# Second products of logits and indexer scores over all 128 partitions

## The chip, the cores and the metric

The kernel runs on one core of a Trainium2 chip. The metric is the device time of one execution in microseconds (us); the time of the kernel before is the median of three runs. TensorE is called PE, VectorE DVE, ScalarE ACT, GpSimd POOL and SyncE SP; PEld is PE's loading of weights.

## The reference

One transformer block: a half feed-forward, a mix of two attentions with gates, another half feed-forward. 512 tokens, width 1024, 8 + 8 heads of 64, an indexer of 4 heads of 64. All is in float32. The part that the change touches is the dot products of queries and keys:

```python
dots = jnp.einsum('bqhd,bsd->bqhs', qib, k_idx_f) * (IDX_DIM ** -0.5)   # indexer, 4 heads
...
logits = jnp.einsum('bqhd,bqkhd->bqhk', qb, k_sel).astype(jnp.float32) * scale   # DSA, 8 heads
...
logits = jnp.einsum('bqhd,bqhjld->bqhjl', qc, k_g).astype(jnp.float32) * scale   # MoBA, 8 heads
```

q and k of both attentions are normalised per head (a root mean square over the 64 elements, times a gain). The indexer's scores select min(256, 512/4) = 128 keys for each query of the DSA attention.

## The kernel before, in words

Every float32 product is made of products of split numbers: a value is a high part (rounded to the short format that PE takes at full rate) and a low part (the rest). A 128-token tile of weights times activations thus takes three products, lines 118 to 120 in `mm3`.

The program goes through feed-forward 1, the mix, and feed-forward 2. PE's order is the order in which the code is written. DVE, ACT and POOL get their order from a scheduler, and then work through it strictly in turn. In the mix, `attention` is a generator that is woven with a *filler* (the projections of later pairs of heads, the gates): after each step of the attention the filler may put one to three `mm3` triples in between (`weave`). The MoBA attention (`br` = 1) runs first, with the indexer's scores (`score`) among its steps; then comes a phase with gates and branch products alone, during which DVE still selects the keys (`topk`); then the DSA attention (`br` = 0).

A step of an attention is a head and a tile of 128 queries (`qt` 0 to 3), 32 steps in each. `logits(i)` makes two products into one PSUM tile `s` (two buffers), line 577 and line 578. A head has 64 elements, so two heads share a tile of 128 partitions. In `q` each head has a slot of its own over all 128 partitions: the high part in the head's own half, the low part in the other half. `k` has the head's high part in both halves, so that line 577 sums q high times k high and q low times k high over 128 partitions. The keys' low parts `kl` lie with both heads in one tile, and line 578 takes one half of the partitions alone, of `q` and of `kl`. The columns are at least 256: 256 (qt 0 and 1), 384 or 512. Lines 503 and 504 do the same for the 12 scores, with `ki[0]` for line 577's `k` and `ki[1]`, which holds the low part in both halves, for `kl`.

What follows a logits tile is a chain over the engines: DVE adds the bias (L583), ACT takes the exponential (L75, through `table_op`), DVE takes the reciprocal and scales (L586, L587), PE transposes (L595, in `turn`, one step of `weave` later), ACT and DVE split the transposed tile (L603, L604), and PE multiplies with the values (L614, L615). DVE also makes the bias with the mask (L559), the selection (L523 to L527), the factors of the norms (L411 to L418, L438, L439) and the keys' low parts (L445). POOL splits the weights (L109).

Lines that the prediction names:

- L118, L119, L120: the three products of a weight tile, all over 128 partitions; L109: POOL's split of weights.
- L577, L578 (`logits`) and L503, L504 (`score`): the two products of each logits or score tile.
- L595: transposes of `turn`; L614, L615: products with the values.
- L445 (`k_post`): the keys' low parts; tag `kl`, two buffers, which gates 3 and 4 of the DSA mix take over later (L669 in `gate`).
- L534, L222: POOL's memsets at the start.

Of the kernel before, what the change touches and what calls it, by code (L numbers as in the profile page):

```python
# [16 lines left out]
P = 128  # L17
# [10 lines left out]
NF = F // P  # L28
# buffers; steps of the filler ahead of the attention (DSA, MoBA) and gates among the filler
TMPS, RAWS = 7, 3  # L30
AHEAD_A, AHEAD_B, GATES, GATES_B = 16, 12, 7, 3
# the step of the MoBA attention that the selection of each query tile follows; a score tile every so many steps
PIN, EVERY = (0, 20, 28, 31), 2
# steps from a product of k or q to the sums of its norm
LAG, LAG_Q = 11, 4
# products that keep the array busy at the start; how far the softmax goes before other work
SPIN, HURRY = 10, 200
# columns of w_in and its units of 128 of them, as kernel() lays them out
C_QA, C_KA, C_VA, C_QB, C_KB, C_VB, C_QI, C_KI, C_G = 0, 512, 1024, 1536, 2048, 2560, 3072, 3328, 3396
# [6 lines left out]
def f32(ap):  # L46
    return ap.bitcast(F32)
# [3 lines left out]
def block_kernel(ctx, tc, x, gains, wgu1, wd1, w_in, w_v, wb_a, wb_b, w_out, wgu2, wd2, rel_bias, onehot, out):  # L51
# [12 lines left out]
    def table_op(kind, *a, **k):  # L64
        """an activation whose table set is loaded once for all neighbours that it serves"""
        def after(prior, make):
            op = make()
            for x in prior:
                tc.add_manual_dep(op.ins, x.ins.name, NOSYNC, reason="table set")
            return op  # L70

        if group["kind"] != kind:
            prior, group["kind"], group["ops"], group["load"] = group["ops"][-16:], kind, [], None
            group["load"] = after(prior, lambda: nc.scalar.preload_act_table_set(kind))
        op = after([group["load"]], lambda: nc.scalar.activation(*a, **k))  # L75
        group["ops"].append(op)
        return op
# [24 lines left out]

# [1 line left out]
    def wtiles(n):  # L104
# [21 lines left out]
    def together(gens):  # L126
        """the products of several tiles, contraction tile by contraction tile"""
        for _ in zip(*gens):
            pass
        for g in gens:  # L130
            run(g)
# [18 lines left out]

# [1 line left out]
    ident = cp.tile([P, P], F32, name="ident")  # L152
# [5 lines left out]

    # keeps the array's clock up until the first data is there
    idle = tmp()[:, 0:P]  # L160
# [9 lines left out]
    nc.gpsimd.memset(epst, EPS)  # L170
    # columns QA, KA, QB, KB; q carries the scale 1/8 and a sign, k the -0.5 of its norm
    gqk = cp.tile([P, 4], F32, name="gqk")
# [6 lines left out]
    def rev(a):  # L179
        """the columns of a [128, 512] tile, back to front within each block of 128"""  # L180
        o = a[:, P - 1:P]
        return bass.AP(o.tensor, o.offset, [list(o.ap[0]), [P, NQ], [-1, P]])
# [5 lines left out]

# [1 line left out]
    def scaled(c, g0, src):  # L190
# [20 lines left out]
    def rsqrt_parts(v):  # L211
        """y near (v + eps)^-0.5 and b = (v + eps) y^2; the root is -0.5 (b - 3) y, one Newton step on."""
        y, b = tmp(), tmp()
        log_exp(y, v, AF.Ln, bias=epst)
        log_exp(y, y, AF.Exp, scale=-0.5)
        nc.scalar.activation(b, y, AF.Square)
        nc.vector.scalar_tensor_tensor(b, v, EPS, b, op0=ALU.add, op1=ALU.mult)
        return y, b
# [10 lines left out]

# [1 line left out]
    PARTS = ((0, 8), (8, 8), (16, 6))  # L231
# [3 lines left out]
    def ffn(xs, wgu, wd, after, lead, halves=whole):  # L235
        """lead() runs the products of the first tiles and returns the root of the norm"""
        tiles = []
# [36 lines left out]

# [1 line left out]
    xs1 = []  # L276
    ss1 = T("os", 1)

    def lead1(tiles, start, begun):
        """four tiles at once, as the parts of x and of the weights come in"""  # L280
        ws = []
# [23 lines left out]

# [1 line left out]
    tab = cp.tile([NB + 1, 16], F32, name="tab")  # L307
# [30 lines left out]

# [1 line left out]
    steps = [0]  # L340
# [52 lines left out]
    def q_post(p, gain, dst):  # L393
        """back to front by blocks and not normalised; a head's high part in its half of the partitions,
        its low part in the other; the norm's factors and their reciprocals, queries on partitions"""
        sq = tmp()
# [24 lines left out]
        later(LAG_Q, norm)  # L421

    def k_post(p, gain, dst):
        """a head's high part in both halves of the partitions, and the low parts of both heads in one more tile"""
        k1 = tmp()
        nc.vector.tensor_mul(k1, p, r2)
        sq = tmp()
        sh, sl = tmp(F32R), tmp(F32R)
        nc.scalar.activation(sh, k1, AF.Square)
        nc.gpsimd.tensor_mul(sq, k1, k1)  # L430
        nc.gpsimd.tensor_sub(sl, sq, f32(sh))

        def norm():
            p2 = mmps()
            nc.tensor.matmul(p2, bd, sh, start=True, stop=False)
            nc.tensor.matmul(p2, bd, sl, start=False, stop=True)
            y, b = rsqrt_parts(p2)
            nc.vector.scalar_tensor_tensor(b, b, -3.0, y, op0=ALU.add, op1=ALU.mult)  # L438
            nc.vector.tensor_mul(y, k1, b)  # L439
            k, low = T("k", 2, (P, 2, S), F32R), T("kl", 2, (P, S), F32R)  # L440
            for e, h1 in enumerate(HALF):
                g = gain[h1]
                for h2 in HALF[e], HALF[1 - e]:
                    nc.scalar.activation(k[h2, e, :], y[h1, :], AF.Copy, scale=g)
                nc.vector.scalar_tensor_tensor(low[h1, :], y[h1, :], g, f32(k)[h1, e, :],  # L445
                                               op0=ALU.mult, op1=ALU.subtract)
            dst.extend([k, low])

        later(LAG, norm)

    def v_units(br, j, dsts, bank=mmps):
        """v of two pairs of heads, tokens on partitions;
        [key tile][head of the pair] has 64 columns of high parts, then 64 of low ones"""
        vs = []
# [34 lines left out]

# [1 line left out]
    ki = [T("a", 16, (P, S), F32R) for _ in range(2)]  # L491
# [5 lines left out]
    def score(qt, hd):  # L497
        W = P * (qt + 1)
        acc = work[:, WOFF[qt]:WOFF[qt] + W]
        b = HALF[hd % 2]  # L500
        q = qi[hd][:, qt * P:(qt + 1) * P]
        p = sps()
        nc.tensor.matmul(p[:, 0:W], q, ki[0][:, 0:W], start=True, stop=False)  # L503
        nc.tensor.matmul(p[:, 0:W], q[b], ki[1][b, 0:W], start=False, stop=True)  # L504
        rl = tmp()
# [22 lines left out]

# [1 line left out]
    PTW = 1664  # L530
# [7 lines left out]
    def attention(br, pairs, outs, extra):  # L538
        """yields how many products of the filler may go in between"""
        sel = br == 0  # L540
# [9 lines left out]
        def addend(i):  # L550
            """bias and mask, over the factor that the sums of products still need"""
            if i < 32:
# [11 lines left out]
        def logits(i):  # L564
# [5 lines left out]
            e = hd % 2  # L570
            b = HALF[e]
            (q, f, _), (k, kl), _ = pairs[hd // 2]
# [4 lines left out]
            nc.tensor.matmul(p[:, 0:N], qb, k[:, e, 0:N], start=True, stop=False)  # L577
            nc.tensor.matmul(p[:, 0:N], qb[b], kl[b, 0:N], start=False, stop=True)  # L578
            addend(i + 1)
# [74 lines left out]

# [1 line left out]
    wide = []  # L656

    def gate(gi, keep):
        """kept until it is used, some of them where a pair of heads had its q or k"""
        def post(p):  # L660
            if gi in (3, 4):
                g1 = T("kl", 2)
            elif gi in (5, 6):
# [16 lines left out]

# [1 line left out]
    moba, dsa = ([([], [], []) for _ in range(4)] for _ in range(2))  # L682
# [21 lines left out]
    nc.vector.tensor_copy(r2T, p[:, 0:NQ])  # L704
    # of the queries, back to front, for both heads of a pair; and its square
    r2q = cp.tile([P, 2, 2 * NQ], F32, name="r2q")
# [56 lines left out]

# [1 line left out]
    def lead2(tiles, start, begun):  # L765
# [22 lines left out]
def _units(w, cols=None, n=P):  # L788
    """[rows, columns] as [unit of n columns, partition, rows of the unit by tiles of 128]"""
    cols = range(0, w.shape[1], n) if cols is None else cols  # L790
    return np.stack([w[:, c:c + n].reshape(-1, P, n).transpose(1, 0, 2).reshape(P, -1) for c in cols])
# [34 lines left out]
```

## Time and profile before

| | |
|---|---|
| median of 3 runs | 1178.36 us (1177.1 to 1178.37) |
| span of the profiled execution | 1176.5 us |
| PE busy | 1163.6 us (99%), 5356 products |
| DVE busy | 700.3 us (60%) |
| POOL busy | 532.4 us (45%) |
| ACT busy | 468.8 us (40%) |
| HBM | 92 GB/s over the span |

The page gives the span alone for the profiled execution, no time of its own; the runs lie 0.6 to 1.9 us above that span. A product's time in the trace runs from its start to a modelled end, and neighbours overlap; what a product costs PE is the distance from its start to the next one's start. "issue" after an idle time means that the engine waited for nothing that the profile shows. The attention stages lie between 420 and 541 us (MoBA) and between 613 and 730 us (DSA).

### The profile page before, as it was taken

What the parts mean: (1) busy time and instruction counts of PE and PEld (TensorE: products, weight loads), DVE (VectorE), ACT (ScalarE), POOL (GpSimd) and SP (SyncE); (2) the same over time, 40 slices, a digit from 0 to 9 for tenths busy, and PEclk for the clock granted to TensorE, in tenths of its full rate; (3) what the DMA queues carried; (4) which work ended last, traced back from release to release, by engine and by line L of the source; (5) the groups of instructions that cost most, each with busy time, mean ns of one, the idle gap of its engine ahead of it and who ended that gap; (6) DMA issues with size and microseconds to landing.
All of it is one profiled execution on the core that took longest, in us unless ns stands there. A gap on an engine that the chain in (4) does not pass through costs nothing.

```text
span 1176.5 us, 14070 instructions
## 1 busy us (share of the span) xinstructions
PE 1163.6 (99%) x5356; PEld 946.2 (80%) x5356; DVE 700.3 (60%) x1075; ACT 468.8 (40%) x757; POOL 532.4 (45%) x280
## 2 busy tenths in 40 slices
PE   9999999999999999999999999999999999999998
PEld 7778888888888878768877767778888888888887
DVE  5863165514655678799979896665665146622651
ACT  6422222312244667657337665433422223222221
POOL 2444454444544655654462422443554444544442
PEclk9999999999999999999999999989999999999999
DMA  7233323323233221221241221322323223232222
GB/s 233 93 109 91 107 90 100 97 92 106 81 83 105 99 82 46 88 63 55 89 135 63 75 69 36 101 96 90 108 90 99 98 90 108 90 104 93 92 88 90
DMA packets 38171, 109.59 MB, mean 93 GB/s; under 512 B 4214, under 2 KB 8664, under 8 KB 38104
## 3 DMA queue, kind: packets, MB, share of 16 engines
q1 hardware_dynamic: 37960, 108.67, 28.9%
q8 instruction: 42, 0.69, 0.2%
q14 instruction: 25, 0.20, 0.1%
q10 hardware_dynamic: 144, 0.02, 0.0%
HBM read 106.54 MB, written 2.14 MB: 92 GB/s over the span
## 4 chain that ended last, share of the span: by engine, by line
PE 93%; DVE 4%; issue 1%; POOL 1%; ACT 1%; DMA 0%; SPq 0%; POOLq 0%; ACTq 0%; DVEq 0%
PE mm L118 22%; PE mm L119 21%; PE mm L120 21%; PE s L118 7%; PE s L119 7%; PE s L120 7%; PE s L578 2%; PE pt L595 1%; PE o L614 1%; PE o L615 1%; PE s L577 1%; POOL wlo L109 1%; PE pt L408 0%; DVE fq L415 0%; DVE kl L445 0%
## 5 line engine op out<-in xcount | busy, mean ns | idle before, releaser
L109 POOL TENSOR_TENSOR wlo<-raw,whi 128x1024 fp32r<-128x1024 f32 (+2 forms) x199 | 467.1, 2349 | 532.1 <-ACT whi L108 529.8
L108 ACT ACTIVATE whi<-raw 128x1024 fp32r<-128x1024 f32 (+2 forms) x207 | 205.0, 993 | 529.3 <-PE mm L119 294.0
L118 PE MATMUL mm<-x,whi 128*128 128x512 f32 x632 | 258.8, 410 | 0.6 <-ACT whi L108 0.6
L120 PE MATMUL mm<-x,wlo 128*128 128x512 f32 x632 | 246.9, 391 | 0.0
L119 PE MATMUL mm<-x,whi 128*128 128x512 f32 x632 | 246.7, 390 | 0.0
L119 PE MATMUL mm<-a,whi 128*128 128x512 f32 (+1 forms) x462 | 178.7, 387 | 0.3
L118 PE MATMUL mm<-a,whi 128*128 128x512 f32 (+1 forms) x462 | 178.6, 386 | 0.0
L120 PE MATMUL mm<-a,wlo 128*128 128x512 f32 (+1 forms) x462 | 178.5, 386 | 0.0
L118 PEld LDWEIGHTS mm<-x,whi 128*128 128x128 f32 x632 | 118.8, 188 | 33.4 <-issue 7.5
L120 PEld LDWEIGHTS mm<-x,wlo 128*128 128x128 f32 x632 | 118.6, 188 | 26.1 <-DVE wlo L109 0.6
L118 PE MATMUL s<-x,whi 128*128 128x512 f32 x352 | 137.0, 389 | 0.6 <-ACT tmp L75 0.6
L119 PE MATMUL s<-x,whi 128*128 128x512 f32 x352 | 137.0, 389 | 0.0
L120 PE MATMUL s<-x,wlo 128*128 128x512 f32 x352 | 137.0, 389 | 0.0
L119 PEld LDWEIGHTS mm<-x,whi 128*128 128x128 f32 x632 | 118.9, 188 | 20.0 <-issue 0.5
L271 DVE SCALAR_TENSOR_TENSOR h<-mm,h 128x512 f32<-128x512 f32 (+1 forms) x49 | 33.3, 681 | 165.3 <-PE mm L120 165.3
L262 DVE TENSOR_TENSOR tmp<-tmp,tmp 128x512 f32<-128x512 f32 x44 | 99.0, 2250 | 29.6 <-ACT tmp L75 29.4
L146 DVE TENSOR_TENSOR a<-tmp,a 128x512 fp32r<-128x512 f32 x49 | 88.5, 1806 | 31.9 <-ACT a L145 31.8
L119 PEld LDWEIGHTS mm<-a,whi 128*128 128x128 f32 x462 | 86.8, 188 | 18.6 <-DVE a L146 1.1
L118 PEld LDWEIGHTS mm<-a,whi 128*128 128x128 f32 x462 | 86.9, 188 | 17.8
L120 PEld LDWEIGHTS mm<-a,wlo 128*128 128x128 f32 x462 | 86.8, 188 | 17.6
L562 POOL TENSOR_SCALAR l<-bias,fq 128x128 f32<-128x128 f32 (+3 forms) x40 | 42.8, 1073 | 78.8 <-PE pt L595 63.0
L118 PEld LDWEIGHTS s<-x,whi 128*128 128x128 f32 x352 | 66.0, 188 | 14.9 <-ACT tmp L75 1.0
(166 smaller groups left out, 1438.9 us busy)
## 6 DMA issues: line engine op xcount, KB each, us to landing
raw<-in_ffn_w_gu_dram SPq DMA_DIRECT2D x84, 512.0 KB, 3.4
raw<-in_w_in_dram SPq DMA_DIRECT2D x35, 512.0 KB, 3.4
raw<-in_ffn_w_down_dram SPq DMA_DIRECT2D x32, 512.0 KB, 3.6
raw<-in_ffn_w_down_dram SPq DMA_DIRECT2D x16, 384.0 KB, 3.1
bias<-fd SPq DMA_DIRECT2D x16, 256.0 KB, 3.4
raw<-in_w_v_dram SPq DMA_DIRECT2D x8, 512.0 KB, 3.4
raw<-in_w_out_dram SPq DMA_DIRECT2D x8, 512.0 KB, 3.4
h<-in_x_dram SPq DMA_DIRECT2D x8, 256.0 KB, 4.2
```

The source lines that it names most:

```text
L108: nc.scalar.activation(hi, raw, AF.Copy)
L109: eng.tensor_sub(lo, raw, f32(hi))
L118: nc.tensor.matmul(pt, wh, xh, start=start, stop=False)
L119: nc.tensor.matmul(pt, wh, xl, start=False, stop=False)
L120: nc.tensor.matmul(pt, wl, xh, start=False, stop=stop)
L146: nc.vector.tensor_sub(lo, src, f32(hi))
L262: nc.vector.tensor_mul(g1, g1, s)
L271: nc.vector.scalar_tensor_tensor(h[c][:, b], pd, 0.5, h[c][:, b], op0=ALU.mult, op1=ALU.add)
L562: nc.gpsimd.tensor_scalar(tms[i], b, inv, None, op0=ALU.mult)
L577: nc.tensor.matmul(p[:, 0:N], qb, k[:, e, 0:N], start=True, stop=False)
L578: nc.tensor.matmul(p[:, 0:N], qb[b], kl[b, 0:N], start=False, stop=True)
L595: nc.tensor.transpose(pp[:, kt * P:(kt + 1) * P], pe[:, kt * P:(kt + 1) * P], ident)
```

## The change

The keys' low parts get two tiles that stay for the whole program, `low0` and `low1`, with a slot of 512 columns for each head of a pair. POOL fills with zeros, once, the half of the partitions that is not the head's own. `k_post` takes the two tiles in turn and writes a head's low part into its half of its slot. The second product of `logits` then takes the head's whole slot of `q` and of `low`, and the second product of `score` takes the whole of `q` and of `ki[1]`, so that here q low times k low is added, which was not computed before. Gates 3 and 4 get a tag of their own, `g`, with two buffers. The memory set aside for the descriptors of dynamic DMAs is cut to 1024; what is left of the diff drops comments. Line numbers of the changed kernel are 6 or so higher than before.

```diff
@@
+    lows = [cp.tile([P, 2, S], F32R, name=f"low{i}") for i in range(2)]
+    for low in lows:
+        for e in range(2):
+            nc.gpsimd.memset(f32(low)[HALF[1 - e], e, :], 0.0)
+    turns = [0]
...
@@ k_post
-            k, low = T("k", 2, (P, 2, S), F32R), T("kl", 2, (P, S), F32R)
+            k, low = T("k", 2, (P, 2, S), F32R), lows[turns[0] % 2]
+            turns[0] += 1
...
-                nc.vector.scalar_tensor_tensor(low[h1, :], y[h1, :], g, f32(k)[h1, e, :],
+                nc.vector.scalar_tensor_tensor(low[h1, e, :], y[h1, :], g, f32(k)[h1, e, :],
@@ score
-        b = HALF[hd % 2]
...
-        nc.tensor.matmul(p[:, 0:W], q[b], ki[1][b, 0:W], start=False, stop=True)
+        nc.tensor.matmul(p[:, 0:W], q, ki[1][:, 0:W], start=False, stop=True)
@@ logits
-            b = HALF[e]
...
-            nc.tensor.matmul(p[:, 0:N], qb[b], kl[b, 0:N], start=False, stop=True)
+            nc.tensor.matmul(p[:, 0:N], qb, kl[:, e, 0:N], start=False, stop=True)
@@ gate
-                g1 = T("kl", 2)
+                g1 = T("g", 2)
@@ kernel
-    nc = bacc.Bacc("TRN2", target_bir_lowering=False, num_devices=1)
+    nc = bacc.Bacc("TRN2", target_bir_lowering=False, num_devices=1, dynamic_dma_scratch_size=1024)
```

PE, ACT and SP keep their order, instruction by instruction. Two places differ. On DVE, near the end of the DSA attention, the multiplication of gate 4 (`kl_6219`, then `g_6217`, out of the PSUM tile `mm`) stands among the softmax of the last two steps; `st` and `l` are the softmax's sums and rows. Before:

```order
L583 ISA l_6179,st_6207<-s_6202,l_6179,fq_5827 128x384
L583 ISA st_6207 128x1
L586 RECIPROCAL st_6207<-st_6207 128x1
L604 TENSOR_TENSOR pt_2634<-pt_6215,pt_2633 128x128
L587 TENSOR_SCALAR l_6179<-l_6179,st_6207 128x384
L583 ISA l_6205,st_6237<-s_6234,l_6205,fq_5827 128x512
L583 ISA st_6237 128x1
L669 TENSOR_TENSOR kl_6219<-mm_6141,R_2731 128x512
```

And in the changed kernel:

```order
L589 ISA l_6177,st_6205<-s_6200,l_6177,fq_5825 128x384
L589 ISA st_6205 128x1
L675 TENSOR_TENSOR g_6217<-mm_6139,R_2737 128x512
L592 RECIPROCAL st_6205<-st_6205 128x1
L610 TENSOR_TENSOR pt_2640<-pt_6213,pt_2639 128x128
L593 TENSOR_SCALAR l_6177<-l_6177,st_6205 128x384
L589 ISA l_6203,st_6235<-s_6232,l_6203,fq_5825 128x512
L589 ISA st_6235 128x1
```

The multiplication has moved five instructions ahead, from behind the bias of the last step to behind that of the step before it. On POOL, at the very start of the program, the zeros stand between the constants and the memsets of `pt`; this is the changed kernel:

```order
L170 MEMSET epst 128x1
L174 TENSOR_SCALAR gqk<-gT 128x1 x4
L308 MEMSET tab 33x16
L426 MEMSET low_2627 64x512 x2
L426 MEMSET low_2628 64x512 x2
L541 MEMSET pt_2637 128x128
L541 MEMSET pt_2638 128x128
L541 MEMSET pt_2639 128x128
L541 MEMSET pt_2640 128x128
L222 MEMSET tmp_307 128x128
L109 TENSOR_TENSOR wlo_336<-raw_334,whi_335 128x1024
```

Four memsets have come in, ahead of the memset of L222 and of the first split of weights; the rest of POOL's order is as it was.

## Rows read from the trace of the kernel before

**Rows 1.** Busy time by stretch of the attention: window, length, PE, PEld, DVE, ACT, POOL, clock
```profile
420.00:498.50 78.50, 78.40 (x399) 58.64 (x398) 61.62 (x157) 54.31 (x126) 47.18 (x34) 1.00 0.21 68
498.50:541.00 42.50, 41.97 (x198) 30.77 (x198) 40.74 (x120) 24.12 (x52) 25.17 (x18) 1.00 0.21 62
613.40:623.20 9.80, 9.80 (x45) 7.17 (x45) 8.11 (x21) 7.05 (x18) 3.00 (x2) 1.00 0.29 105
623.20:695.90 72.70, 69.20 (x367) 53.54 (x367) 67.37 (x161) 50.85 (x111) 28.51 (x17) 1.00 0.20 66
695.90:730.00 34.10, 34.10 (x162) 26.02 (x163) 25.67 (x65) 18.89 (x40) 7.79 (x4) 1.00 0.15 47
```
**Rows 2.** Chain of work that ended last, 672.8 to 696: start, us, what
```profile
673.32 2.15 DVE l L559
...
695.87 0.30 PE pt L595
```
**Rows 3.** Same stretches, instructions on the tile s alone: PE (x two per pair), PEld, DVE, ACT
```profile
420.00:498.50 78.50, 21.01 (x62) 11.50 (x62) 11.24 (x21) 4.18 (x10) 1.00 0.21 68
498.50:541.00 42.50, 9.13 (x26) 4.82 (x26) 6.18 (x11) 1.66 (x3) 1.00 0.21 62
613.40:623.20 9.80, 2.50 (x8) 1.29 (x7) 2.18 (x4) 0.00 (x0) 1.00 0.29 105
623.20:695.90 72.70, 13.53 (x40) 7.43 (x40) 10.12 (x19) 0.00 (x0) 1.00 0.20 66
695.90:730.00 34.10, 5.41 (x16) 2.96 (x16) 5.09 (x9) 0.00 (x0) 1.00 0.15 47
```
**Rows 4.** Line 578: its products in ns (min/median/max), PEld's idle time before its loads
```profile
L578 PE MATMUL s<-kl,q x64: 379/410/501, 420.7 to 721.8; 64*128 64x256 f32 x32, 64*128 64x384 f32 x16, 64*128 64x512 f32 x16
...
  issue: 16.5, 58
```
**Rows 5.** PE in order of time, a score tile and a logits tile: start, us, what
```profile
440.98 0.28 PE L503 MATMUL s<-a,a 128*128 128x256 f32 x1
...
441.83 0.39 PE L119 MATMUL mm<-x,whi 128*128 128x512 f32 x1
...
442.29 0.39 PE L577 MATMUL s<-k,q 128*128 128x512 f32 x1
442.62 0.49 PE L578 MATMUL s<-kl,q 64*128 64x512 f32 x1
443.04 0.50 PE L118 MATMUL mm<-x,whi 128*128 128x512 f32 x1
443.37 0.39 PE L119 MATMUL mm<-x,whi 128*128 128x512 f32 x1
```
**Rows 6.** PE in order of time, products with the values, two of each width
```profile
445.04 0.40 PE L614 MATMUL o<-pt,v 128*128 128x512 f32 x1
...
445.50 0.34 PE L614 MATMUL o<-pt,v 128*128 128x384 f32 x1
...
445.86 0.28 PE L614 MATMUL o<-pt,v 128*128 128x256 f32 x1
...
446.09 0.28 PE L614 MATMUL o<-pt,v 128*128 128x256 f32 x1
```
**Rows 7.** PEld in order of time, loads for the logits tile of rows 5
```profile
442.61 0.18 PEld L578 LDWEIGHTS s<-kl,q 64*128 64x128 f32 x1 [0.36 <-issue]
...
443.14 0.19 PEld L119 LDWEIGHTS mm<-x,whi 128*128 128x128 f32 x1
```
**Rows 8.** POOL in order of time, the start of the program
```profile
4.66 0.65 POOL L534 MEMSET pt<- 128x128 f32 x4
8.87 0.20 POOL L222 MEMSET tmp<- 128x128 f32 x1 [3.56 <-DVE os L204]
```
**Rows 9.** DVE in order of time, end of the DSA attention
```profile
717.36 0.75 DVE L559 SCALAR_TENSOR_TENSOR l<-bias,fq,work 128x512 f32<-128x512 f32 x1 [0.80 <-PE pt L595]
...
721.68 0.16 DVE L586 RECIPROCAL st<-st 128x1 f32<-128x1 f32 x1 [1.77 <-ACT l L75]
```

## The prediction

> **What bounds the kernel now.** I read first the busy time by stretch over the two attentions, since only there the edited products run. The reader is to see that PE is busy almost without a break: of the five stretches it idles 0.10, 0.53, 0, 3.50 and 0 us (length less busy time), at full clock [rows 1]. So a product that takes PE less time should bring the end forward by as much. But DVE is a close second. Its idle time in the same stretches is 16.9, 1.8, 1.7, 5.3 and 8.4 us [rows 1]. The chain of work shows what that means: from 673.32 to 695.87 us it starts on DVE and comes back to PE only at the end [rows 2], and almost all pieces between are DVE's. There PE was not the bound, it just had enough filler to look busy. I call the stretches A (420 to 498.5), B (498.5 to 541), C (613.4 to 623.2), D (623.2 to 695.9) and E (695.9 to 730). A and B are the MoBA attention, with B holding the selection on DVE; C to E are the DSA attention.
>
> **What the change takes off PE.** The tile s gets two products per logits or score tile, and PE has 62, 26, 8, 40 and 16 instructions on it in A to E [rows 3]: 31, 13, 4, 20 and 8 pairs, 76 in all, which are the 64 of L578 and the 12 of L504. What one pair costs is read from starts, not from durations: a 64-row product shows 379 to 501 ns, and PEld idles 16.5 us before 58 of its 64 loads, 0.28 us each [rows 4], but both overlap with neighbours. For a tile of 512 columns, from L577's start to the start of the product behind the next one it is 443.37 less 442.29, 1.08 us for three products (0.33, 0.42 and 0.33 us each) [rows 5]. Products over 128 rows with fresh weights each, two into one tile, step by (445.50 - 445.04) / 2 = 0.23 us at 512 columns, 0.18 at 384 and 0.115 at 256 [rows 6]. Three of 512 would take 0.69 us, so 0.39 us is lost: 0.10 on the way into the 64-row product, 0.19 at it, 0.10 behind the next. For a score tile of 256 columns it is 441.83 less 440.98 = 0.85 us [rows 5], against 2 x 0.115 + 0.23 = 0.46: again 0.39. Since the loss does not grow with the columns, I take it for 384 too. The second product over 128 rows has the form of L577 (type, weights, columns); zeros stream like other numbers. So PE is relieved of 76 x 0.39 = 29.6 us, in A to E 12.1, 5.1, 1.6, 7.8 and 3.1.
>
> The bound from below for this term is the load of weights. In rows 7 the load for L578 idles 0.36 us and starts at 442.61, beside its own product, while the load for L119 starts at 443.14, with L118's product of 443.04 [rows 5] still running over the same 128 rows. Loads ahead under full-height products are thus what this kernel does all the time, and I take the whole 0.39. The Trainium skill, page "TensorE: Matmul & The Clock Gate", section "Part 3: Packing small matmuls — row/col tiling", speaks against it: it says that a weight load overlaps products in flight only when its row group differs. The trace does not agree with that as it stands (rows 7). By that rule the second product's load would come into the open.
>
> **What it adds and moves.** Each of these I cost at nothing. The low parts are written by as many DVE instructions of the same shape, and the two tiles alternate as the two buffers of `kl` did, so L445 waits for the same logits as before; were it to wait longer, the softmax queued behind it on DVE would wait, and PE's transposes for that. The four memsets of 64x512: four of 128x128 take 0.65 us, 0.16 each, so one costs between that and four times as much for four times the columns, and all four 0.65 to 2.6 us; POOL then idles 3.56 us before L222, which waits for DVE [rows 8]. That idle time hides them; without it the start would slip by at most 2.6 us. Gate 4's multiplication moves ahead of a reciprocal (L586) that waited 1.77 us for ACT [rows 9]. It takes about the 0.75 us of a 128x512 DVE instruction [rows 9], and its own product ends three PE products (0.7 us) behind the logits of that step, so it fits into that wait. If not, it costs 0.75 us in the last steps' softmax, once. Gates 3 and 4 no longer wait for `kl`, which can only help; I give it nothing. The memory for dynamic DMAs concerns none, as the kernel issues its DMAs on SP and ACT.
>
> **What of 29.6 us reaches the end.** DVE's work stays the same, and the attention ties PE to it step by step, so a stretch cannot shrink by more than DVE's idle time and, since some of that is waiting for ACT inside the chain, not by all of it. D is my gauge: DVE idles 7% of it, and PE already idles 5%.
> - A: relief 12.1, DVE idle 16.9. Afterwards DVE would idle 4.8 of 66.4 us, 7% as in D, so PE would begin to wait; I take 10.5 (bounds 8 and 12.1).
> - B: relief 5.1, DVE idle 1.8, PE idle 0.5. DVE bounds it; I take 1.2 (0 and 5.1).
> - C: relief 1.6, DVE idle 1.7; I take 1.4 (1 and 1.6).
> - D: relief 7.8, DVE idle 5.3, and the chain on DVE for 22.5 us of it; I take 2.8 (0 and 7.8).
> - E: relief 3.1, DVE idle 8.4; I take it all (2 and 3.1).
>
> The sum is 10.5 + 1.2 + 1.4 + 2.8 + 3.1 = 19.0 us, with bounds of 11 and 29.7. Between the attentions and behind them PE finds what it found before, only earlier: DVE's selection comes earlier with the end of the MoBA attention. The sum is made against the span of 1176.5 us and gives 1157.5; the median of the runs lies 1.9 us above the span, so I predict 1178.4 - 19.0 = 1159.4 us.
>
> **Rivals.**
> - *DVE holds nothing back* (0.12): the softmax may lag behind by a step while PE goes on with filler, and DVE catches up after each attention. All 29.6 us arrive: 1148.8 us. For it: PE hardly idles in B although DVE is 96% busy. Against: the chain on DVE in D [rows 2].
> - *DVE holds more back* (0.13): the lower bounds, 11 us, give 1167.4 us, and it goes on to 1176 if A too is bound by DVE.
> - *The loads of weights come into the open* (0.04): the load takes 0.18 to 0.19 us [rows 7], so a pair wins 0.39 - 0.19 = 0.20 us, 15.2 us in all. DVE then takes less back; with the relief halved in A, C and E (6.2, 0.8, 1.6) and the same 1.2 and 2.8 in B and D it is 12.6 us: 1165.8 us. This is what the rule of that page of the Trainium skill would do here. Against it stand rows 7.
> - *The height is not the cause* (0.04): all slow products are at once 64 rows high and the second ones into s, and the pair could be slow for the other reason. Then nothing is won: 1178, or 1181 if the memsets show. Against it: L614 and L615 also go in pairs into one tile, without loss [rows 6].
> - *Slower, as DVE meets POOL more often* (0.05): L559 took 2.15 us in the chain of D [rows 2] and 0.75 in E, for the same shape [rows 9], 1.4 us more. The place is B and D, where POOL has 18 and 17 instructions [rows 1]. With DVE pressed closer, each of them might catch one more DVE instruction of the chain; it decides from 19.0 / 1.4 = 14 more such meetings on, and 20 more would give 1178.4 - 19.0 + 28 = 1187 us. Against it: DVE is already busy 93 to 96% there, and both engines have as many instructions as before. The Trainium skill, page "SBUF — State Buffer", section "Who interferes with whom", says that a DVE instruction with two SBUF inputs and a POOL instruction that reads SBUF block each other; L559 reads two SBUF tiles, and its row agrees with that.
>
> **How the numbers follow.** The forecast, DVE takes about a third back, 1153 to 1166 us, gets 0.62. The first rival's end is the lower end of the range, 1148.5; the upper end is 1168, just past the lower bounds of the sum, so that the part of "holds more back" above it (0.09), "not the cause" and "slower" are left out, 0.18. A measurement of this kernel can tell about 0.2% from no change, 2.4 us. Faster: 0.62 + 0.12 + 0.13 + 0.04 = 0.91; same 0.04; slower 0.05.
>
> **What would show it.** In the changed profile the second products show 128 rows and the duration of the first ones (0.39 us at 512 columns [rows 5]), the step of a 512 tile to the second product behind it falls from 1.08 to 0.69 us, and PEld's "issue" idle time before these loads is gone; if not, the height was not the cause. PE's idle time on DVE grows from 4 us by some 10, in A, B and D; if it stays, the first rival holds. Stretch E and the gates behind it should shift as a block. I am wrong if a product over 128 rows on the same tiles still steps like the 64-row one, or if DVE's own time in B and D changes by more than a few us.

## The result and the profile after

The changed kernel takes 1162.93 us (1162.74 to 1167.82, four runs) against 1178.36 us. The ratio is 0.9882, with a 95% interval of 0.9863 to 0.9901: 1.2% faster, 15.4 us. Forecast were 1159.4 us and a range of 1148.5 to 1168. The execution whose profile is shown here is the slowest of the four, 1167.82 us with a span of 1166.0 us, 5 us above the others: its mean granted clock was 0.992, theirs 0.998 to 0.999, and PE's clock fell in it at two places where it had not fallen in the profile of before (last section).

The products behave as forecast. PE in order of time, a score tile and a logits tile of the changed kernel, to be held against [rows 5]:

```profile
424.80 0.28 PE L510 MATMUL s<-a,a 128*128 128x256 f32 x1
...
425.27 0.39 PE L119 MATMUL mm<-x,whi 128*128 128x512 f32 x1
...
425.73 0.40 PE L583 MATMUL s<-k,q 128*128 128x512 f32 x1
425.96 0.39 PE L584 MATMUL s<-low,q 128*128 128x512 f32 x1
426.19 0.39 PE L118 MATMUL mm<-x,whi 128*128 128x512 f32 x1
426.42 0.39 PE L119 MATMUL mm<-x,whi 128*128 128x512 f32 x1
```

From the first product to the second one behind the tile it is 426.42 less 425.73 = 0.69 us (before 1.08), and 0.47 us for the score tile (before 0.85). PEld shows why nothing is left over:

```profile
425.50 0.19 PEld L583 LDWEIGHTS s<-k,q 128*128 128x128 f32 x1
425.73 0.19 PEld L584 LDWEIGHTS s<-low,q 128*128 128x128 f32 x1
```

The second product's weights are loaded from 425.73 on, while the first product, which starts at the same moment, runs over the same rows.

Then the busy time by stretch (columns as in [rows 1]), with the borders at the PE instructions at which A to E begin and end before:

```profile
420.00:489.30 69.30, 67.10 (x400) 58.22 (x399) 59.96 (x152) 52.34 (x122) 46.54 (x34) 1.00 0.23 77
489.30:529.50 40.20, 37.59 (x198) 30.88 (x197) 39.74 (x121) 24.43 (x54) 23.40 (x18) 1.00 0.21 66
604.40:612.70 8.30, 8.30 (x46) 7.05 (x46) 6.65 (x16) 6.67 (x17) 3.00 (x3) 1.00 0.34 122
612.70:688.50 75.80, 65.37 (x369) 55.33 (x367) 70.89 (x166) 50.64 (x112) 28.05 (x17) 0.95 0.20 63
688.50:719.50 31.00, 31.00 (x163) 26.05 (x162) 25.39 (x65) 18.39 (x40) 7.87 (x4) 1.00 0.17 52
```

A is 9.2 us shorter, B 2.3, C 1.5 and E 3.1, but D is 3.1 us longer, and the stretch between the attentions grew from 72.4 to 74.9 us: 10.5 in all, the difference of the two spans. The medians differ by 15.4; the clock that PE lost at those two places, some 5 us by the rows of the last section, makes up the rest (an estimate). PE, which idled 0.1, 0.5 and 3.5 us in A, B and D, now idles 2.2, 2.6 and 10.4. Who it waits for in the changed kernel (total in us, times, longest):

```profile
PE pt L601 <- DVE pt L610: 12.0, 10, 2.6
PE pt L601 <- DVE l L593: 1.8, 1, 1.8
...
PE pt L601 <- DVE st L592: 1.2, 1, 1.2
```

Nearly all of it is transposes of the softmax that wait for DVE, 15.0 us. In the kernel before it was 4.0 us:

```profile
PE pt L595 <- DVE pt L604: 2.6, 3, 1.9
PE pt L595 <- DVE l L587: 1.4, 1, 1.4
```

What DVE did then is seen where its rows stand beside POOL's. DVE in order of time in D of the changed kernel:

```profile
662.95 2.85 DVE L566 SCALAR_TENSOR_TENSOR l<-bias,fq,work 128x512 f32<-128x512 f32 x1
...
675.70 2.36 DVE L415 TENSOR_TENSOR fq<-fq 128x8 f32<-128x8 f32 x1
...
685.64 2.54 DVE L593 TENSOR_SCALAR l<-l,st 128x256 f32<-128x256 f32 x1
```

POOL in the same stretch:

```profile
662.88 2.38 POOL L109 TENSOR_TENSOR wlo<-raw,whi 128x1024 fp32r<-128x1024 f32 x1 [3.88 <-ACT whi L108]
...
675.63 2.40 POOL L109 TENSOR_TENSOR wlo<-raw,whi 128x1024 fp32r<-128x1024 f32 x1 [6.57 <-ACT whi L108]
...
685.66 2.36 POOL L109 TENSOR_TENSOR wlo<-raw,whi 128x1024 fp32r<-128x1024 f32 x1 [0.67 <-ACT whi L108]
```

Each DVE instruction begins within 0.1 us of a POOL split of weights and ends 0.03 to 0.54 us after it; that is what is called a meeting here. One of the three has only 8 columns; the form of the first, 512 columns, took 0.75 us elsewhere [rows 9]. Behind two of the three, PE then waits:

```profile
667.91 0.44 PE L601 MATMUL pt<-ident,l 128*128 128x128 f32 x1 [2.63 <-DVE pt L610]
...
688.32 0.41 PE L601 MATMUL pt<-ident,l 128*128 128x128 f32 x2 [1.79 <-DVE l L593]
```

DVE counts as busy while it is held, so its 93% of D (70.89 of 75.8 us) were not 93% of work. How much it is can be summed from the traces: over both attentions and what lies between them (420 us to the end of E), the DVE instructions that run beside a split and take over 0.2 us more than the shortest of their form lose 27.0 us (20 instructions) before and 30.6 us (21) in the changed kernel; in D alone 10.6 and 14.2 us, eight instructions each time. That is what the experiments go after.

### The profile page after: what moved, and what is told of

The parts are those of the page before. It is cut to its first block, busy times and chain, and to the rows that moved or that the text cites. A ratio compares the mean times of both kernels' runs of the same rounds, so it can differ in the third digit from the quotient of the medians.

```text
span 1166.0 us, 14074 instructions
## 1 busy us (share of the span) xinstructions
PE 1141.1 (98%) x5356; PEld 949.4 (81%) x5356; DVE 701.4 (60%) x1075; ACT 467.3 (40%) x757; POOL 532.8 (46%) x284
## 4 chain that ended last, share of the span: by engine, by line
PE 83%; DVE 9%; ACT 3%; issue 3%; POOL 1%; DMA 0%; SPq 0%; POOLq 0%; ACTq 0%; DVEq 0%
PE mm L120 20%; PE mm L118 20%; PE mm L119 20%; PE s L118 7%; PE s L119 7%; PE s L120 7%; DVE l L566 1%; DVE l L589 1%; POOL wlo L109 1%; DVE l L593 1%; DVE pt L610 1%; PE pt L601 1%; ACT l L75 1%; DVE low L453 1%; PE o L620 1%
## 5 line engine op out<-in xcount | busy, mean ns | idle before, releaser
L109 POOL TENSOR_TENSOR wlo<-raw,whi 128x1024 fp32r<-128x1024 f32 (+2 forms) x199 | 466.2, 2344 | 541.4 <-ACT whi L108 536.4
L118 PE MATMUL mm<-x,whi 128*128 128x512 f32 x632 | 253.0, 400 | 0.7 <-ACT whi L108 0.7
L119 PE MATMUL mm<-x,whi 128*128 128x512 f32 x632 | 247.3, 391 | 0.0
L262 DVE TENSOR_TENSOR tmp<-tmp,tmp 128x512 f32<-128x512 f32 x44 | 99.0, 2250 | 29.6 <-ACT tmp L75 29.4
L120 PEld LDWEIGHTS s<-x,wlo 128*128 128x128 f32 x352 | 66.1, 188 | 13.8
```

The costliest lines, as they stand in the source:

```text
L109: eng.tensor_sub(lo, raw, f32(hi))
L118: nc.tensor.matmul(pt, wh, xh, start=start, stop=False)
L119: nc.tensor.matmul(pt, wh, xl, start=False, stop=False)
L120: nc.tensor.matmul(pt, wl, xh, start=False, stop=stop)
L262: nc.vector.tensor_mul(g1, g1, s)
```

## The experiments

**Is it the height of the products, or the rest of the edit?** The changed kernel with all its new tiles, but both second products over half the partitions:

```diff
-            nc.tensor.matmul(p[:, 0:N], qb, kl[:, e, 0:N], start=False, stop=True)
+            b = HALF[e]
+            nc.tensor.matmul(p[:, 0:N], qb[b], kl[b, e, 0:N], start=False, stop=True)
```

(and the like in `score`).

> The changed kernel with all its new tiles, zeros, memsets, the tag of the gates and the order on DVE, but both second products (logits and scores) over the head's own 64 partitions again. Theory 'height of the product': everything of the gain comes from the 128 rows, so the time is that of the kernel before, 1176 to 1180 us, and the step from the first product of a 512 tile to the second one behind it is 1.08 us again. Rival 'tiles and order': if the new tiles, the gates' own tag or the moved DVE instruction brought a part, the time stays at 1163 to 1172 us.

Measured: 1176.31 us, a ratio of 0.999 (0.9979 to 1.0) to the kernel before. Line 586 is its second product:

```profile
L586 PE MATMUL s<-low,q x64: 379/410/498, 420.6 to 722.2; 64*128 64x256 f32 x32, 64*128 64x384 f32 x16, 64*128 64x512 f32 x16
...
  issue: 16.5, 58
```

Durations and PEld's idle time are those of [rows 4], and the step of the first 512-column tile of [rows 5] is 443.31 less 442.22, 1.09 us, as before. The height is the cause; tiles, zeros, memsets and the moved multiplication are worth nothing that can be told, as costed.

**The scores alone.** The kernel before with only this:

```diff
-        nc.tensor.matmul(p[:, 0:W], q[b], ki[1][b, 0:W], start=False, stop=True)
+        nc.tensor.matmul(p[:, 0:W], q, ki[1][:, 0:W], start=False, stop=True)
```

> The kernel before with only the 12 score products over 128 partitions. Theory 'DVE gives back by stretch': the scores lie between 426 and 514 us, nearly all in stretch A, where DVE had 16.9 us idle, so nearly all of 12 x 0.39 = 4.7 us arrives: 1173.5 to 1175 us. Rival 'PE's relief is mostly lost anywhere in the attentions' (half of it, as in the whole change): 2.4 us, 1176 us.

Measured: 1174.38 us against 1177.0, ratio 0.9978 (0.9966 to 0.9991), so 1.1 to 4 us. The sign is settled. By the interval 2.4 us would do and 4.7 would not, but the runs (1172.1 to 1176.6) differ in their granted clock: compared at the same clock (0.995, 0.997, 0.999 and 1.0) this kernel is 3.5 to 4.2 us ahead, nearer to 4.7. So most of the relief arrives here; how much exactly is not settled.

**Less work for DVE.** The softmax's last scaling on ACT, before and after:

```diff
-                nc.vector.tensor_scalar(pe, pe, st[:, 2:3], None, op0=ALU.mult)
+                nc.scalar.activation(pe, pe, AF.Copy, scale=st[:, 2:3])
```

> The kernel before with the softmax's last scaling (L587, 64 instructions of 0.28 to 0.48 us or more) on ACT in place of DVE; it computes the same. Both theories: PE is the bound here and idles only 4.1 us on DVE, so at most that is won: 1174 to 1178 us; a longer chain over ACT could cost a few us instead. It is the partner of e4_after_act.

> The changed kernel with the softmax's last scaling on ACT in place of DVE; it computes the same. Theory 'DVE's work holds the gain back': DVE loses some 26 us of work in the two attentions, so more of the 29.6 us arrives than the 15.4 measured: against e3_before_act the change wins 22 to 28 us, 1150 to 1156 us. Rival 'the chain of a softmax step is too long for PE's order, whoever does the work': the step goes through ACT, which is not faster, so the change wins no more than 15 us against e3_before_act and the time stays at 1161 to 1166 us.

Measured: 1184.02 and 1164.25 us, ratios 1.0053 (1.0033 to 1.0073) and 0.9888 (0.9868 to 0.9909). The first is a miss: the move costs the kernel before 6 to 7 us. The change wins 19.8 us here, more than 15.4 and less than 22, so neither theory has it, though the time itself lies where the rival put it. PE's waits in the second one:

```profile
PE pt L601 <- DVE pt L610: 9.4, 6, 2.6
PE pt L601 <- DVE st L592: 5.0, 2, 3.8
```

They are about as long as in the changed kernel: less work on DVE did not end them. The edit does more than move work, though: the scheduler then puts what is left on DVE in another order, in some hundred places of the two traces. With the scaling on ACT in the DSA attention alone:

> The changed kernel with the softmax's last scaling on ACT in the DSA attention alone, on DVE in the MoBA attention; it computes the same. In e4_after_act PE gained 8.6 us over the DSA attention against the kernel before, where the changed kernel gained 1.7, and 2 to 4 us less over the MoBA attention. Theory 'each attention has its own tight engine': the better of the two in each place gives 1155 to 1160 us. Rival 'the shift between the attentions decides, not DVE's work': the DSA attention does not keep e4's gain when it starts at another time, 1162 to 1165 us.

Measured: 1160.84 us, ratio 0.9856 (0.9838 to 0.9873), 0.8 us above what the theory expected and below the rival's range. The interval overlaps that of the changed kernel (0.9863 to 0.9901), so whether this is faster is not shown.

Since ACT got the work there, the next pair leaves it out: the scaling (L587 before, L593 in the changed kernel) is deleted, so the probabilities stay unnormalised.

> The kernel before without the softmax's last scaling (L587 left out, so the probabilities stay unnormalised): 64 instructions less on DVE, none more elsewhere. Both theories: PE is the bound and idles 4.1 us, so 1173 to 1177 us. It is the partner of e7_after_noscale.

> The changed kernel without the softmax's last scaling (left out as in e6_before_noscale). Theory 'DVE's work holds the gain back': with some 26 us less on DVE the change wins 22 to 28 us against e6_before_noscale, 1148 to 1154 us. Rival 'something else than DVE (PE's order, ACT, the two buffers of s) holds it back': it wins 15 us as before, 1159 to 1162 us.

Measured: 1179.04 us, ratio 1.0004 (0.9993 to 1.0015), and 1154.37 us, ratio 0.9798 (0.9783 to 0.9813). The kernel before wins nothing, 2 us outside what was expected, and the change wins 24.7 us. That is the theory's number: what DVE has to do between PE's steps held the gain back. DVE's order differs here too from the kernels that the pair was made from, in the same way for both, so the pair does not show the work alone. What PE waits for DVE's split of the transposes (in the changed kernel 12.0 us) without the scaling, before and after:

```profile
PE pt L594 <- DVE pt L603: 1.0, 2, 0.6
```

```profile
PE pt L600 <- DVE pt L609: 4.9, 5, 1.8
```

**Without most of the meetings of DVE and POOL.** DVE keeps all its work; POOL writes zeros in place of the weights' low parts between the two feed-forwards (`steps[0]` is above 0 there alone), in 0.96 us for 1024 columns instead of some 2.4. These low parts are thus left out. The edit, cut to its core:

```diff
-        wsplit(raw, hi, lo)
+        if steps[0]:
+            nc.scalar.activation(hi, raw, AF.Copy)
+            nc.gpsimd.memset(f32(lo), 0.0)
+        else:
+            wsplit(raw, hi, lo)
```

> The changed kernel in which, between the two feed-forwards, POOL fills the weights' low parts with zeros in place of computing them (63 weight tiles; the low parts are left out there, so POOL reads no SBUF for them). DVE has the same instructions. Theory 'meetings of DVE and POOL are a good part of DVE's time': the instructions of DVE that took some 2 us for 0.2 to 0.7 (34 us over both attentions in the changed kernel) shrink, PE waits less, 1150 to 1157 us. Rival 'the meetings only fill time that DVE had': 1161 to 1164 us.

> The kernel before in which, between the two feed-forwards, POOL fills the weights' low parts with zeros in place of computing them (left out as in e9_after_nosplit, which took 1140.8 us). Theory 'DVE, kept by its meetings with POOL, holds the gain back': without the meetings all of the 29.6 us arrives, so this kernel takes 1168 to 1172 us. Rival 'the meetings cost the kernel before as much as the changed one': the change wins 15 us here too, 1155 to 1158 us.

Measured: 1140.75 us, ratio 0.9683 (0.9666 to 0.97), for the changed kernel, and 1167.86 us, ratio 0.9915 (0.9897 to 0.9934), for the one before. The first is 9 us below what was expected, the second just below. They ran beside different runs of before; the ratios differ by 0.0232, 27 us of the 29.6. PE, DVE and ACT go through the same instructions in the same order here as in the kernels that they were made from (compared in the traces), and so they do in the next pair; the scheduler's order is no rival. The scaling (line 593 in the changed kernel, line 598 here, ns as min/median/max) shows what went:

```profile
L593 DVE TENSOR_SCALAR l<-l,st x64: 266/463/2536, 422.1 to 715.3; 128x128 f32<-128x128 f32 x16, 128x256 f32<-128x256 f32 x16, 128x384 f32<-128x384 f32 x16, 128x512 f32<-128x512 f32 x16
```

```profile
L598 DVE TENSOR_SCALAR l<-l,st x64: 276/416/1120, 423.1 to 693.9; 128x128 f32<-128x128 f32 x16, 128x256 f32<-128x256 f32 x16, 128x384 f32<-128x384 f32 x16, 128x512 f32<-128x512 f32 x16
```

Some holding is left: the DVE instructions beside the zeros lose 2.9 us (6 instructions, summed as above). PE's waits for transposes fall from 15.0 us to one row:

```profile
PE pt L606 <- DVE pt L615: 2.4, 3, 1.5
```

That 1140.75 lies below the 1148.8 us of the first rival has its reason at the end of the mix, where the attentions are over. PE in order of time in the kernel before, and the busy time of that stretch (PE second, its clock behind POOL):

```profile
765.11 0.47 PE L118 MATMUL mm<-k,whi 128*128 128x512 f32 x1 [1.49 <-DVE tmp L741]
767.07 0.80 PE L120 MATMUL mm<-k,wlo 128*128 128x512 f32 x1 [1.25 <-POOL wlo L109]
```

```profile
765.00:775.00 10.00, 8.64 (x25) 6.59 (x26) 7.13 (x5) 2.21 (x3) 4.38 (x2) 0.66 0.34 113
```

The same stretch of the changed kernel, 10 us earlier:

```profile
755.00:765.00 10.00, 8.75 (x26) 6.85 (x26) 6.49 (x5) 2.21 (x3) 3.74 (x2) 0.66 0.30 105
```

Two waits (2.7 us) and a fallen clock (3.4 us) cost about 6 us there in both profiled executions; in executions with a higher mean clock it is less. Without POOL's splits they are gone from both. That is half or more of the 9.5 us that the kernel before won; most of the rest is its 4.0 us of waits for transposes, of which 0.3 are left.

**Shorter meetings.** Nothing left out: POOL's split in four instructions, all but that of the first tiles of feed-forward 1.

```diff
-        wsplit(raw, hi, lo)
+        n = src.shape[1] // 4
+        nc.scalar.activation(hi, raw, AF.Copy)
+        for c in (slice(i * n, (i + 1) * n) for i in range(4)):
+            nc.gpsimd.tensor_sub(lo[:, c], raw[:, c], f32(hi)[:, c])
```

> The kernel before with POOL's split of weights in four pieces, as in e10_after_pieces; it computes the same. PE is the bound here, so it wins at most PE's 4 us of idle time on DVE: 1173 to 1178 us. The change then wins 22 to 29 us against it if a meeting lasts as long as POOL's instruction, 15 us if the sum counts.

> The changed kernel with POOL's split of each weight tile (L109, some 2.35 us) in four instructions of a quarter of the columns, except for the first tiles of feed-forward 1; it computes the same. Theory 'a meeting lasts as long as the POOL instruction': DVE is held for at most some 0.6 us at a time, most of e9's gain comes without leaving anything out, 1145 to 1155 us. Rival 'what counts is how long POOL reads in sum': DVE is held four times as often for a quarter, 1161 to 1164 us.

Measured: 1166.78 us, ratio 0.9903 (0.9887 to 0.992), and 1144.82 us, ratio 0.9717 (0.9698 to 0.9736). Before wins 6 us more than expected (again in good part the end of the mix), and the change is worth 22.0 us on top. The page of the second one: busy time, and POOL's pieces:

```profile
PE 1131.6 (99%) x5356; PEld 946.0 (83%) x5356; DVE 563.5 (49%) x1075; ACT 467.1 (41%) x757; POOL 686.6 (60%) x881
...
L117 POOL TENSOR_TENSOR wlo<-raw,whi 128x256 fp32r<-128x256 f32 (+2 forms) x796 | 619.7, 810 | 386.0 <-ACT whi L115 381.9
```

POOL works 154 us more than in the changed kernel (532.8), and DVE, with the same 1075 instructions, is busy 138 us less (701.4). The scaling's longest instruction halves:

```profile
L596 DVE TENSOR_SCALAR l<-l,st x64: 268/478/1320, 420.9 to 698.7; 128x128 f32<-128x128 f32 x16, 128x256 f32<-128x256 f32 x16, 128x384 f32<-128x384 f32 x16, 128x512 f32<-128x512 f32 x16
```

Summed as above, DVE now loses 12.5 us beside splits in 32 instructions, at most 0.58 us in one, against 30.6 us in 21 and 2.22 at most. So DVE is held more often and for less: the rival, that the sum of POOL's reads counts, falls, and so does the thought that POOL only had to have more time to spare. PE still waits 6.0 us for transposes here, against 1.0 in e11_before_pieces: that is 5 of the 7.6 us that do not arrive. Both moves together:

> The changed kernel with both: the split in four pieces and the softmax's scaling on ACT in the DSA attention; it computes the same. If the pieces already free DVE, the move to ACT adds nothing or lengthens the step: within 2 us of e10_after_pieces. If the sum of POOL's reads counts, it is 2 us below e10_after_pieces, as e5_after_act_dsa was below the changed kernel.

Measured: 1143.01 us, ratio 0.9706 (0.9685 to 0.9727), 1.8 us below e10_after_pieces; the intervals overlap, so this does not tell whether the move to ACT still adds something. It is the fastest version measured that computes all of the reference, 2.9% below the kernel before.

## Why the prediction was right, and where it missed

- *76 pairs of 0.39 us.* Right: 0.69 and 0.47 us stand in the trace for 0.69 and 0.46, and 27 of the 29.6 us arrive where DVE is hardly held. PE's waits for transposes were forecast to grow from 4 us by some 10; they grew from 4.0 to 15.0.
- *The load of weights.* The rival fell: the loads run under full-height products (the load of 425.73 above). The Trainium skill, page "TensorE: Matmul & The Clock Gate", section "Part 3: Packing small matmuls — row/col tiling", has the sentence that a load overlaps products in flight only when its row group differs; as it stands, this trace does not agree with it.
- *The height as the cause.* Right, by e1_half_rows.
- *What is added costs nothing.* Right within that run's interval. The four memsets take 2.20 us, and POOL still waits for DVE behind them:

```profile
4.77 2.20 POOL L426 MEMSET low<- 64x512 f32 x4
8.51 0.20 POOL L222 MEMSET tmp<- 128x128 f32 x1 [0.95 <-DVE os L204]
```

- *DVE gives back about a third.* The direction was right and the size too small: 14.2 of 29.6 us did not arrive, against 10.6. The term that was mis-sized is D, 2.8 us forecast. In the profiled execution D grew by 3.1 us; a clock of 0.95 over 75.8 us is 3.8 us of PE's time, so without that D would have won 0.7 us at most (an estimate from that row). A came out 1.3 us short, B 1.1 better, so these two nearly cancel; C and E came as forecast.
- *The chain in D.* [rows 2] was read as a chain on DVE for 22.5 us that comes back to PE only at the end. Summed over its pieces, DVE has 15.5 of the 22.5 us, and in the middle the chain runs over PE for more than 3 us (rows below). So DVE is the largest part of this chain, not nearly all of it. That DVE leads in D stands without it, by the waits above.

```profile
677.57 0.30 PE pt L595
...
680.80 0.23 PE pt L595 x2
```

- *DVE's idle time as the limit.* This was the gauge. As a rule of thumb it came near in A, C and E; B shrank by 2.3 us, more than the 1.8 that DVE idled, and D not at all. What it left out is what the prediction gave only to the rival that ends slower: DVE's busy time was partly time in which POOL held it. The rival's mechanism is real and its sign was wrong. The change brought one more meeting, not fourteen (27.0 us in 20 instructions before, 30.6 in 21 after); those that were there already decided how fast DVE could follow. In D they got longer by 3.6 us, and DVE's busy time there grew by as much (67.37 to 70.89 us), which is at the edge of what the prediction named as a sign of being wrong. The Trainium skill, page "SBUF — State Buffer", section "Who interferes with whom", calls the port pair that DVE shares with POOL an exclusive lock and says that whoever issues first gets it for the whole instruction while the other blocks. The three pairs of rows above agree with the length of such a block (2.85, 2.36 and 2.54 us beside 2.38, 2.40 and 2.36), and so does the gain from shorter POOL instructions; who issued first the rows tell for two of the pairs, while in the third DVE's row begins 0.02 us ahead of POOL's.
- *Between the attentions nothing changes.* Missed by 2.5 us in the profiled execution: 0.7 us of PE's waiting and 1.8 us of fallen clock lie there (530 to 550 us, last section).

## What to carry to other kernels

In this kernel a product over half the rows between full-height ones cost 0.39 us more than a full one: in such a place, pad its operand with zeros if the other operand's rows are there anyway. When PE gets faster, look at what feeds it next, and ask of that engine's busy time how much is work: compare the longest with the shortest duration of one form. If a second engine's long instructions hold it, cut those into pieces before moving work away; here that gave more than the change itself.

## What the hardware showed unexpectedly

PE's clock fell in the profiled execution of the changed kernel at three places. One is the end of the mix, as in the kernel before; these are the other two (busy time by stretch, the clock behind POOL):

```profile
530.00:550.00 20.00, 19.33 (x123) 17.88 (x122) 18.48 (x52) 15.94 (x31) 5.84 (x4) 0.91 0.12 41
660.00:680.00 20.00, 17.37 (x81) 14.43 (x81) 16.82 (x35) 12.70 (x28) 5.38 (x3) 0.83 0.16 57
```

At 1.2 in place of 2.4 GHz for a part of the time, PE lost 1.8 and 3.4 us of clock there. Windows of finer cut put the second fall at 666.9 to 673.7 us (clock 0.50), so it began within PE's longest wait, the 2.63 us that end at 667.91. In the kernel before it fell at the end of the mix, at the two waits shown above (0.66 over 10 us). So a wait may cost twice; that the waits are its cause was not tested.

A POOL subtraction of 256 columns takes 0.85 us on average, a quarter of one of 1024 columns 0.62 (2.48 / 4; both by form, meetings included). Cutting it costs POOL a third more time (619.7 us in all instead of 466.2), and was worth it all the same.
